# Neighbourhood attention: q and k split at their norm, loaded early, four pairs of heads in one sequence

## The chip, the core and the metric

The kernel runs on one core of a Trainium2 chip. The core has a matrix engine (TensorE, PE in the profile, with its weight loads as PEld), a vector engine (VectorE, DVE), a scalar engine (ScalarE, ACT), GpSimd (POOL) and a queue for transfers (SyncE, SP). Each engine works through its own instructions in order and waits for the others at semaphores. The metric is the device time of one execution in microseconds (us), the median of several runs.

## What is computed

Two layers of a hybrid block over 1024 latent tokens (a grid of 16 rows and 64 columns) and 256 context tokens, width 1024, float32. Each layer projects the normed tokens to three branches, runs them, and merges them with gates:

```
h = rms_norm(x, norm_w) * (1 + scale) + shift
(na_q, na_k, na_v, gla_q, gla_k, gla_v, gla_g, ret_q, ret_k, ret_v, z, g) = split_cols(h @ w_in)
na  = neighbourhood_attention(rms_norm(q), rms_norm(k), v, ...)     # 8 heads of 64
gla = bidir_scan(...)   # gated linear attention, 4 heads
ret = bidir_scan(...)   # retention, 4 heads
x = x + gate * merge_branches((na, gla, ret), z, g, w_branch, w_out)
```

In neighbourhood attention each latent token scores 8 rows by 16 columns of keys around it, with a bias from a table, and all 256 context keys, under one softmax:

```
s_win = einsum('bhwd,bhrwcd->bhwrc', q_r, k_win) * scale + bias
s_ctx = einsum('bhwd,bhnd->bhwn', q_r, kc) * scale
p = softmax(concat([s_win, s_ctx]))
o = einsum(p_win, v_win) + einsum(p_ctx, vc)
```

Context tokens attend to the context only; the last layer leaves their output out.

## The kernel before

**Slots.** A class `Drv` (L47) writes the program slot by slot. In each slot it moves the workers on by a step, emits a stretch of projection matmuls (the gemm stream), emits the stores deferred from the slot before and the evacuations of finished products, moves each lane on by a step, and the workers once more. A lane is one long generator, here the attention lane of a layer: retention, then GLA (`gla`, L627), then neighbourhood attention (`na`, L842). A worker is a short one, such as one unit of attention. A stretch has 6144 moving columns times `drv.mult` (L363, L374). So the order on each engine is fixed when the program is written, and a matmul that waits holds all matmuls behind it.

**Products in parts.** A product of float32 operands is made of three fast ones: hi by hi, hi by lo and lo by hi, where hi is the operand cast to the fast format and lo is the operand minus hi. `conv` (L330) splits weights: a cast on ACT (L337), two subtractions on POOL (L340).

**The q and k projections.** `fm` writes a product with 128 features on the partitions and up to 512 tokens in a row, in units of 24 matmuls (12,288 columns at 512 tokens). `qk_evac` (L1129) takes such a product of one pair of heads: copy and square on ACT (L1132, L1133), mean by a matmul (L1138), an inverse root on ACT (L1140 to L1142) with one Newton step on DVE (L1145 to L1160), where the tokens are also put into the order that attention reads. The result `raw` is stored to nq or nk in DRAM (m is 0 for q, 1 for k). There are 24 such evacuations in layer 0 and 20 in layer 1. They run while the lane is in GLA, whose decay differences dd are made on POOL (L775, L776), exponentiated on ACT (L789), multiplied on DVE (L798 to L800) and used by PE (L811). The tiles `nraw`, `nsq`, `nrs` come from `stg` (L144), a ring of eight buffers that the stores of the other stages share.

**Attention.** `na` takes the eight heads as four pairs. `load_v(p)` (L849) fetches the values of a pair into `vw` (four column windows, all row groups) and `vcx` (context). `heads(p)` (L860) first splits q and k of the pair at `drv.mult` 0.3 (`NA_M0`): for each head and each block of 512 or 256 tokens it loads 64 features of k and of q into a tile `nsp`, twice, to partitions 0 to 63 and 64 to 127 (a source with a leading broadcast of two), casts both to hi on ACT (L876) and subtracts on DVE (L879, L881), so that `ks` holds hi of k in both halves, `kl` lo of k, and `qs` hi of q in one half and lo of q in the other. One matmul over 128 partitions (L902) then gives hi by hi plus lo by hi, and one over 64 (L905) adds hi by lo. The lane waits until all of the pair is split (`lane_join(sp)`, L891). I call this the join. `qs`, `ks` and `kl` have one buffer each.

Then the units run at `drv.mult` 0.65, one spawned every second slot: eight windows of 128 latent tokens and, in layer 0, two blocks of context tokens. A unit (`pair`, L969) loads its bias `bt` (two buffers), makes the scores of its two heads (L902, L905), the softmax (DVE and ACT, L920 to L938), transposes the weights (L947, L950), copies them out (L961, L964), multiplies with the values (L999) and copies the result to `oN`, which is stored after four units.

While the lane runs attention, the gemm stream makes the gates g, whose results are stored by `gd<-st_g`.

Of the kernel before, what the change touches and what calls it, by code (L numbers as in the profile page):

```python
# [8 lines left out]
F32 = mybir.dt.float32  # L9
# [25 lines left out]
NA_M0, NA_M1 = 0.3, 0.65  # L35
# [11 lines left out]
class Drv:  # L47
    """Interleaves background work with the stream of projection matmuls, slot by slot."""
# [58 lines left out]
def hybrid_kernel(ctx: ExitStack, tc: tile.TileContext, A: dict, out: bass.AP):  # L107
# [39 lines left out]
    # ------------------------------------------------------------------ activations in hi/lo parts  # L147
# [29 lines left out]
    # ------------------------------------------------------------------ modulation  # L177
# [68 lines left out]
    # ------------------------------------------------------------------ norm of one token tile  # L246
# [47 lines left out]
    # ------------------------------------------------------------------ weights and projections  # L294
# [124 lines left out]
    # ================================================================== layers  # L419
    xcur = [A["x"][t * P:(t + 1) * P, :] for t in range(LT)] + [A["ctx"][t * P:(t + 1) * P, :] for t in range(2)]  # L420
    L = []
    for layer in range(DEPTH):
# [31 lines left out]
        d["nq"] = dt_("nq", [512, NTOK])  # L454
        d["nk"] = dt_("nk", [512, NTOK])
# [5 lines left out]
    # ------------------------------------------------------------------ retention / GLA output tail (one chunk)  # L461
# [43 lines left out]
    # ------------------------------------------------------------------ retention  # L505
# [120 lines left out]
    # ------------------------------------------------------------------ GLA  # L626
# [214 lines left out]
    # ------------------------------------------------------------------ neighbourhood attention  # L841
    def na(layer):  # L842
        d = L[layer]
        ntok, last = d["ntok"], d["last"]
        with tc.tile_pool(name=f"na{layer}", bufs=2) as pn:
            ws = []
            vts = {}

            def load_v(p):  # L849
                vw = pn.tile([P, 16, P], F32, tag="vw", name="vw", bufs=2)  # L850
                vcx = pn.tile([P, 2, P], F32, tag="vcx", name="vcx", bufs=2)
                vts[p] = vw, vcx
                nv = d["nv"][:, p * P:(p + 1) * P]
                for j in range(4):
                    dma(vw[0:4 * NCOL[j], j * 4:j * 4 + 4, :],
                        nv[0:NLAT, :].rearrange("(g c r) d -> (c r) g d", g=4, r=4)[4 * COL0[j]:4 * COL0[j] + 4 * NCOL[j], :, :])
                    yield
                dma(vcx, nv[NLAT:NTOK, :].rearrange("(c p) d -> p c d", p=P))

            def heads(p):  # L860
                drv.mult = NA_M0
                vw, vcx = vts[p]

                def split(hd, t0, nn):
                    hs = slice(64 * hd, 64 * hd + 64)
                    os = slice(64 - 64 * hd, 128 - 64 * hd)
                    pieces = []
                    for src, dst, on in ((d["nk"], ks[hd], True), (d["nq"], qs[hd], t0 < ntok)):
                        if on:
                            st = stg("nsp")  # L870
                            dma(st[:, :nn], src[p * P + 64 * hd:p * P + 64 * hd + 64, t0:t0 + nn].unsqueeze(0).to_broadcast([2, 64, nn]))
                            pieces.append((st, dst[:, t0:t0 + nn]))
                    yield
                    yield
                    for st, dst in pieces:
                        sc.copy(dst, st[:, :nn])  # L876
                    yield
                    yield
                    ve.tensor_tensor(kl[hs, t0:t0 + nn], pieces[0][0][hs, :nn], fv(pieces[0][1][hs]), op=ALU.subtract)  # L879
                    for st, dst in pieces[1:]:  # L880
                        ve.tensor_tensor(dst[os], st[os, :nn], fv(dst[os]), op=ALU.subtract)  # L881

                qs = [pn.tile([P, ntok], F32R, tag=f"q{x}", name=f"q{x}", bufs=1) for x in range(2)]
                ks = [pn.tile([P, NTOK], F32R, tag=f"k{x}", name=f"k{x}", bufs=1) for x in range(2)]
                kl = pn.tile([P, NTOK], F32R, tag="kl", name="kl", bufs=1)
                sp = []
                for t0, nn in blocks(NTOK):
                    for hd in range(2):
                        sp.append(drv.spawn(split(hd, t0, nn)))
                        yield  # L890
                yield from lane_join(sp)  # L891
                yield
                drv.mult = NA_M1
                nxt = load_v(p + 1) if p < 3 else iter(())

                def scores(qc, win):
# [3 lines left out]
                    def prod(outs, kof):  # L900
                        for hd in range(2):
                            pe.matmul(outs[hd], qs[hd][:, qc:qc + P], kof(ks[hd][:]), start=True, stop=False)  # L902
                        for hd in range(2):
                            hs = slice(hd * 64, hd * 64 + 64)
                            pe.matmul(outs[hd], qs[hd][hs, qc:qc + P], kof(kl[hs]), start=False, stop=True)  # L905
# [47 lines left out]
                def evac_t(hd, pts, win):  # L953
# [4 lines left out]
                    if win is not None:  # L958
                        half, j = win
                        cw = 4 * NCOL[j]  # L960
                        ve.tensor_copy(PT[0:cw, 0:384], ptw[0:cw, 0:384])  # L961
                        for i in range(3):
                            ch.append((vw[0:cw, j * 4 + half + i, hs], PT[0:cw, i * P:(i + 1) * P]))
# [5 lines left out]
                def pair(qc, win, dst, after):  # L969
                    bts = [None, None]  # L970
# [10 lines left out]
                    sc_ = scores(qc, win)  # L981
                    yield
                    ps_ = [soft1(sc_[hd], win, bts[hd]) for hd in range(2)]
                    yield
# [8 lines left out]
                    cA, cB = [evac_t(hd, ts[hd], win) for hd in range(2)]  # L993
# [12 lines left out]
                for half in range(2):  # L1006
                    oN = stg("oN")
                    for j in range(4):
# [5 lines left out]
                        ws.append(drv.spawn(pair((half * 4 + j) * P, (half, j), dst, after)))  # L1014
                        yield
                        if half or j > 1:
                            next(nxt, None)
                        yield
                if not last:
                    oN = stg("oNc")  # L1020
                    for cb in range(2):
# [4 lines left out]
                        ws.append(drv.spawn(pair(NLAT + cb * P, None, oN[:, cb * P:(cb + 1) * P], after)))  # L1026
                        yield
                        yield

            drv.mult = NA_M0  # L1030
            yield from load_v(0)
            for p in range(4):
                yield from heads(p)
# [3 lines left out]
    # ------------------------------------------------------------------ projections of one layer  # L1037
# [29 lines left out]
    def projections(layer):  # L1067
# [61 lines left out]
        def qk_evac(p):  # L1129
            def f(m, t0, nn, ps):  # L1130
# [4 lines left out]
                def w():  # L1135
# [25 lines left out]
                    dst = d["nq"] if m == 0 else d["nk"]  # L1161
                    drv.defer(lambda: dma(dst[p * P:(p + 1) * P, t0:t0 + nn], raw[:, :nn]))
# [53 lines left out]
    # ------------------------------------------------------------------ merge and output projection  # L1216
# [116 lines left out]
    # ------------------------------------------------------------------ background lane of one layer  # L1333
# [244 lines left out]
```

## Time and profile before

| | us |
|---|---|
| median of 3 runs | 3232.21 |
| lowest and highest run | 3231.21, 3236.86 |
| span of the profiled execution (first to last instruction) | 3228.6 |
| PE busy in it | 2914.7 |
| DVE, ACT, POOL busy in it | 1518.7, 1065.5, 1006.4 |
| attention stage, layer 0 | about 830 to 1322 |
| attention stage, layer 1 | about 2466 to 2900 |

The profile gives no time of the profiled execution besides its span, which is 3.6 us below the median of the runs. Its rows name an instruction by line, engine and operation, with output and inputs by the names above; `nsp<-nk` is a load of k into the split's tile. A timeline row begins with the start and the duration in us; "x16" is a run of 16 like instructions. SPq is SyncE's queue; a long SPq row is a transfer that could not be handed on at once. The granted clock is that of PE, as a share of full speed.

### The profile page before, as it was taken

To read this page: it belongs to the slowest core of one execution; us is meant where nothing else is said; L and a number is where in the kernel's file an instruction comes from. 1 tells how busy PE (TensorE), PEld (TensorE's weight loads), DVE (VectorE), ACT (ScalarE), POOL (GpSimd) and SP (SyncE) were. 2 spreads that over 40 slices of the span, in tenths; PEclk is the share of its full clock that TensorE was granted. 3 is DMA by queue.
4 is the path that set the end of the run, shared out by engine and by line. 5 is a ranking of instruction groups with operands and counts; after the bars stand their busy time and mean duration, and the time that the engine had idled before them with its cause. 6 is when DMAs were issued, how large, how long until landed. Compare 5 with 4: busy or idle time off the path is not lost.

```text
span 3228.6 us, 49602 instructions
## 1 busy us (share of the span) xinstructions
PE 2914.7 (90%) x18768; PEld 2481.6 (77%) x18768; DVE 1518.7 (47%) x3325; ACT 1065.5 (33%) x2459; POOL 1006.4 (31%) x962
## 2 busy tenths in 40 slices
PE   7999999899586787999999999999998677799999
PEld 5999977788475575777899999987776555577889
DVE  5046578666153354223434236477662444452331
ACT  4123565332143343221113222465332333332220
POOL 4122124455000011242655232124542010024474
PEclk9999999999898898999999999999999888899999
DMA  5244423323233233466435344432332333244633
GB/s 223 90 149 131 146 89 95 102 86 97 81 101 105 74 107 111 144 188 217 155 114 154 96 148 124 142 104 89 113 98 89 105 110 104 85 124 157 211 127 115
DMA packets 343887, 395.39 MB, mean 122 GB/s; under 512 B 28044, under 2 KB 259996, under 8 KB 343648
## 3 DMA queue, kind: packets, MB, share of 16 engines
q1 hardware_dynamic: 343648, 392.22, 38.4%
q8 instruction: 148, 2.42, 0.3%
q14 instruction: 91, 0.75, 0.1%
HBM read 289.54 MB, written 102.58 MB: 121 GB/s over the span
## 4 chain that ended last, share of the span: by engine, by line
PE 72%; DMA 10%; DVE 6%; issue 4%; SPq 4%; POOL 3%; ACT 1%; POOLq 0%; DVEq 0%; ACTq 0%
PE fm L371 30%; PE tm L371 17%; PE mg L371 9%; DMA nsp<-nk 5%; SPq L114 4%; PE gla_lv L811 3%; DMA nsp<-nq 3%; PE na_o L999 2%; PE na_ptw L947 1%; DVE ek L798 1%; DVE eq L799 1%; POOL wlo L340 1%; PE na_sc L902 1%; DVE eq L800 1%; PE na_ptc L950 1%
## 5 line engine op out<-in xcount | busy, mean ns | idle before, releaser
L371 PE MATMUL fm<-h,whi 128*128 128x512 f32 (+1 forms) x3936 | 942.6, 385 | 0.0
L340 POOL TENSOR_TENSOR wlo<-wraw,whi 128x512 fp32r<-128x512 f32 (+1 forms) x336 | 450.6, 1362 | 1415.2 <-ACT whi L337 1345.1
L371 PEld LDWEIGHTS fm<-h,whi 128*128 128x128 f32 x3936 | 685.5, 193 | 153.2 <-issue 29.4
L371 PE MATMUL fm<-h,wlo 128*128 128x512 f32 (+1 forms) x1968 | 472.6, 378 | 0.0
L371 PEld LDWEIGHTS fm<-h,wlo 128*128 128x128 f32 x1968 | 342.9, 191 | 69.1 <-issue 4.3
L371 PE MATMUL tm<-whi,h 128*128 128x256 f32 (+1 forms) x2528 | 346.6, 285 | 2.4 <-ACT h L290 1.7
L371 PEld LDWEIGHTS tm<-whi,h 128*128 128x128 f32 x2528 | 320.7, 189 | 4.0 <-ACT h L290 2.1
L337 ACT CAST whi<-wraw 128x1024 fp32r<-128x1024 f32 (+1 forms) x168 | 175.6, 1048 | 244.4 <-PE tm L371 121.1
L811 PE MATMUL gla_lv<-eq,ek 128*128 128x128 f32 x1008 | 138.3, 281 | 52.1 <-DVE eq L800 51.7
L811 PEld LDWEIGHTS gla_lv<-eq,ek 128*128 128x128 f32 x1008 | 128.2, 193 | 73.8 <-issue 45.7
L775 POOL TENSOR_TENSOR dd<-Ac,ash 128x256 f32<-128x256 f32 x126 | 106.6, 846 | 245.6 <-DVE eq L800 87.5
L371 PE MATMUL tm<-wlo,h 128*128 128x256 f32 (+1 forms) x1264 | 178.1, 283 | 0.0
L371 PEld LDWEIGHTS tm<-wlo,h 128*128 128x128 f32 x1264 | 163.0, 189 | 0.2 <-POOL wlo L340 0.2
L1175 ACT ACTIVATE st_g<-fm 128x512 f32<-128x512 f32 (+1 forms) x120 | 66.3, 553 | 277.1 <-PE fm L371 275.5
L371 PE MATMUL tm<-whi,yy 128*128 128x256 f32 x1152 | 148.1, 280 | 0.0
L371 PEld LDWEIGHTS tm<-whi,yy 128*128 128x128 f32 x1152 | 140.8, 188 | 0.1
L817 DVE COPY_PREDICATED att<-gmask,gla_lv 128x512 f32<-128x512 uint8 x108 | 80.0, 741 | 126.1 <-PE gla_lv L811 126.1
L1191 DVE SCALAR_TENSOR_TENSOR st_z<-st_z,fm 128x512 f32<-128x512 f32 (+1 forms) x60 | 38.0, 633 | 211.7 <-ACT st_z L1190 209.8
L902 PE MATMUL na_sw<-k,q 128*128 128x288 f32 (+1 forms) x128 | 39.7, 381 | 97.3 <-ACT k L876 97.3
L879 DVE TENSOR_TENSOR kl<-nsp,k 64x512 fp32r<-64x512 f32 (+1 forms) x48 | 29.5, 615 | 195.0 <-ACT k L876 195.0
L902 PE MATMUL na_sc<-k,q 128*128 128x256 f32 x144 | 41.6, 361 | 82.5 <-ACT k L876 82.4
L411 DVE COPY st_tm<-tm 128x256 f32<-128x256 f32 (+1 forms) x59 | 25.2, 428 | 171.9 <-PE tm L371 167.6
(1567 smaller groups left out, 4707.1 us busy)
## 6 DMA issues: line engine op xcount, KB each, us to landing
wraw<-in_w_in SPq DMA_DIRECT2D x104, 512.0 KB
wt<-in_w_mod SPq DMA_DIRECT2D x48, 512.0 KB
gd<-st_g SPq DMA_DIRECT2D x96, 256.0 KB
gt<-gd SPq DMA_DIRECT2D x96, 256.0 KB
bt<-in_na_bm SPq DMA_DIRECT2D x32, 384.0 KB
ot<-o SPq DMA_DIRECT2D x48, 256.0 KB
wraw<-in_w_branch SPq DMA_DIRECT2D x24, 512.0 KB
ret<-st_tm SPq DMA_DIRECT2D x78, 128.0 KB
```

Of the source, the lines that this page charges most:

```text
L114: nc.sync.dma_start(dst, src)
L337: sc.copy(hi[:, :, :w], raw[:, :, :w])
L340: gp.tensor_tensor(lo[:, ks, :w], raw[:, ks, :w], fv(hi[:, ks, :w]), op=ALU.subtract)
L371: pe.matmul(ps, a(k), b(k), start=i == 0, stop=i == tot - 1)
L775: gp.tensor_tensor(dv[:, :, Lh:], av[:, :, Lh:], rv, op=ALU.subtract)
L798: ve.tensor_tensor(ek_, E_, kd_, op=ALU.mult)
L811: pe.matmul(pl_[:, h, :], ek_[:, h, :], eq_[:, h, :], start=True, stop=True)
L817: ve.copy_predicated(att, gmask[:, lv, :].unsqueeze(1).to_broadcast([P, 4, P]), pl_)
L902: pe.matmul(outs[hd], qs[hd][:, qc:qc + P], kof(ks[hd][:]), start=True, stop=False)
L999: pe.matmul(po[64 * hd:64 * hd + 64, 0:P], ch[i][0], ch[i][1], start=i == 0, stop=i == n - 1)
L1175: sc.activation(st[:, :nn], ps, AF.Tanh, scale=0.5)
L1191: ve.scalar_tensor_tensor(st[:, :nn], st[:, :nn], 1.0, ps, op0=ALU.add, op1=ALU.mult)
```

## The change

The split moves from attention to `qk_evac`. After the Newton step the result is cast to hi on ACT into the tile of `rs`, POOL subtracts it to lo in place in `raw`, and the parts are stored: for q a tensor of [pair, head, 128, tokens] with hi in the head's own 64 rows and lo in the others (four stores), for k one tensor of hi and one of lo (two stores). Two steps lie between the Newton step and the stores that were not there.

`heads` no longer splits. k of a pair is loaded whole: `k0` and `k1`, each with the leading broadcast of two over 64 rows of 1280 tokens, and `kl` without one, two buffers each. q is loaded by each unit, 128 tokens of both heads, three buffers. The values of a window are loaded by each unit too, after its scores, in the three row groups that it uses, four buffers; before, 16 groups were loaded a pair and are shared by two units. `both(p)` loads k and vcx of a pair: the first pair's before any unit, seven slots at the multiplier that GLA leaves (1.0), those of pair p + 1 after units 3, 4 and 5 of pair p. There is no join; units of all four pairs follow each other, one every second slot, at 0.65.

```diff
-        d["nq"] = dt_("nq", [512, NTOK])
-        d["nk"] = dt_("nk", [512, NTOK])
+        d["nq"] = dt_("nq", [4, 2, P, NTOK])
+        d["nkh"] = dt_("nkh", [512, NTOK])
+        d["nkl"] = dt_("nkl", [512, NTOK])
...
+            def load_k(p):
+                ks = []
+                for hd in range(2):
+                    k = pn.tile([P, NTOK], F32R, tag=f"k{hd}", name=f"k{hd}", bufs=2)
+                    r = p * P + 64 * hd
+                    dma(fv(k[:]), d["nkh"][r:r + 64, :].unsqueeze(0).to_broadcast([2, 64, NTOK]))
+                    ks.append(k)
+                    yield
+                kl = pn.tile([P, NTOK], F32R, tag="kl", name="kl", bufs=2)
+                dma(fv(kl[:]), d["nkl"][p * P:(p + 1) * P, :])
+                tiles["k", p] = ks, kl
...
-                sp = []
-                for t0, nn in blocks(NTOK):
-                    for hd in range(2):
-                        sp.append(drv.spawn(split(hd, t0, nn)))
-                        yield
-                yield from lane_join(sp)
-                yield
-                drv.mult = NA_M1
-                nxt = load_v(p + 1) if p < 3 else iter(())
...
+                def load_vw(win):
+                    half, j = win
+                    cw = 4 * NCOL[j]
+                    vw = pn.tile([P, 3, P], F32, tag="vw", name="vw", bufs=4)
+                    dma(vw[0:cw], d["nv"][0:NLAT, p * P:(p + 1) * P].rearrange("(g c r) d -> (c r) g d", g=4, r=4)
+                        [4 * COL0[j]:4 * COL0[j] + cw, half:half + 3, :])
+                    return vw
...
                 def pair(qc, win, dst, after):
+                    q = pn.tile([P, 2, P], F32R, tag="q", name="q", bufs=3)
+                    dma(fv(q[:]), d["nq"][p, :, :, qc:qc + P].rearrange("h d t -> d h t"))
...
-            drv.mult = NA_M0
-            yield from load_v(0)
+            for _ in both(0):
+                yield
+            for _ in range(4):
+                yield
+            drv.mult = NA_M1
             for p in range(4):
-                yield from heads(p)
+                nxt = both(p + 1) if p < 3 else iter(())
+                for n, unit in enumerate(heads(p)):
+                    ws.append(drv.spawn(unit))
+                    yield
+                    if n > 2:
+                        next(nxt, None)
+                    yield
+                for _ in nxt:
+                    pass
...
-                    dst = d["nq"] if m == 0 else d["nk"]
-                    drv.defer(lambda: dma(dst[p * P:(p + 1) * P, t0:t0 + nn], raw[:, :nn]))
+                    hi, lo = rs.bitcast(F32R)[:, :nn], raw.bitcast(F32R)[:, :nn]
+                    yield
+                    sc.copy(hi, raw[:, :nn])
+                    yield
+                    gp.tensor_tensor(lo, raw[:, :nn], rs[:, :nn], op=ALU.subtract)
+
+                    def store():
+                        ts = slice(t0, t0 + nn)
+                        if m == 0:
+                            for hd in range(2):
+                                hs, os = slice(64 * hd, 64 * hd + 64), slice(64 - 64 * hd, 128 - 64 * hd)
+                                dma(d["nq"][p, hd, hs, ts], fv(hi[hs]))
+                                dma(d["nq"][p, hd, os, ts], fv(lo[hs]))
+                        else:
+                            dma(d["nkh"][p * P:(p + 1) * P, ts], fv(hi))
+                            dma(d["nkl"][p * P:(p + 1) * P, ts], fv(lo))
+                    drv.defer(store)
```

The transfers on SyncE, before, at the first join of layer 0 (wraw is a weight half, gd the store of a gate):

```order
L114 DMA nsp_8569<-nk_0_106 128x1x512
L114 DMA nsp_8571<-nq_0_105 128x1x512
L114 DMA nsp_8579<-nk_0_106 128x1x512
L114 DMA nsp_8581<-nq_0_105 128x1x512
L114 DMA wraw45_8583<-in_w_in 128x4x256
L114 DMA gd_0_99<-st_g_8561 128x256
L114 DMA nsp_8594<-nk_0_106 128x1x512
L114 DMA nsp_8596<-nq_0_105 128x1x512
L114 DMA nsp_8606<-nk_0_106 128x1x512
L114 DMA nsp_8608<-nq_0_105 128x1x512
```

Two more pairs of 256 tokens follow; the pair's first scores stand on PE after the first of these loads and need all of the tiles. After the change, on SyncE, from the bias of unit 3 to that of unit 5 of the first pair:

```order
L114 DMA bt<-in_na_be 128x2x288 [waits DMAHW2_49,DVE_49]
L114 DMA k_9007<-nkh_106 128x1x1280 [waits DMAHW3_49]
L114 DMA gd_99<-st_g 128x512 [waits DMAHW4_49,Activation_49]
L114 DMA vw<-nv_104 96x3x128 [waits DMAHW5_49]
L114 DMA q<-nq_105 128x2x128 [waits DMAHW6_49,PE_49]
L114 DMA bt<-in_na_be 128x2x288 [waits DMAHW7_49,DVE_49]
L114 DMA wraw_9075<-in_w_in 128x4x256 [waits DMAHW0_49,Pool_49]
L114 DMA gd_99<-st_g 128x256 [waits DMAHW1_49,Activation_49]
L114 DMA k_9100<-nkh_106 128x1x1280 [waits DMAHW2_49]
L114 DMA vw<-nv_104 96x3x128 [waits DMAHW3_49,PE_49]
L114 DMA q<-nq_105 128x2x128 [waits DMAHW4_49,PE_49]
L114 DMA bt<-in_na_bm 128x2x384 [waits DMAHW5_49,DVE_49]
```

The loads of the next pair's k now stand among the loads of the running units, and a transfer waits for the one eight issues earlier (the counters DMAHW0 to DMAHW7 are used in turn): the second vw here waits for the first k.

PE at the change of pairs in layer 1, before, from the last scores of the first pair (fm is the gemm stream, na_ptw and na_ptc the transposes, na_o the values' product):

```order
L371 MATMUL fm<-h_4_16236,wlo_23913 128x512 x4
L371 MATMUL fm<-h_0_16239,whi_23778 128x512 x4
L902 MATMUL na_sw<-k_24389,q_24387 128x288
L902 MATMUL na_sw<-k_24390,q_24388 128x288
L905 MATMUL na_sw<-kl,q_24387 128x288
```

After it:

```order
L371 MATMUL fm<-h_4_16285,wlo_23930 128x512 x4
L985 MATMUL na_o<-PT,vw 64x128 x6
L985 MATMUL na_o<-PT,vcx 64x128 x4
L877 MATMUL na_sw<-k_24106,q 128x288
L877 MATMUL na_sw<-k_24199,q 128x288
```

Before, 26,624 columns of gemm stand between the last scores of one pair and the first of the next, and the last units have run out; now 8,192 stand there, as between any two units, and the unit before last of the old pair is still on its way.

POOL in the q and k stage of layer 0, before:

```order
L775 TENSOR_TENSOR dd<-Ac_5549,ash 128x64x4
L776 TENSOR_TENSOR dd<-ash,Ac_5549 128x64x4
L340 TENSOR_TENSOR wlo_5809<-wraw_5602,whi_5808 128x2x256 x2
L775 TENSOR_TENSOR dd<-Ac_5549,ash 128x128x2
L776 TENSOR_TENSOR dd<-ash,Ac_5549 128x128x2
```

After it:

```order
L1160 TENSOR_TENSOR nraw<-nraw,nrs 128x512
L776 TENSOR_TENSOR dd<-Ac_5595,ash 128x64x4
L777 TENSOR_TENSOR dd<-ash,Ac_5595 128x64x4
L1160 TENSOR_TENSOR nraw<-nraw,nrs 128x256
L340 TENSOR_TENSOR wlo_5867<-wraw_5649,whi_5866 128x2x256 x2
L776 TENSOR_TENSOR dd<-Ac_5595,ash 128x128x2
L777 TENSOR_TENSOR dd<-ash,Ac_5595 128x128x2
L1160 TENSOR_TENSOR nraw<-nraw,nrs 128x512 x2
```

The new subtractions (L1160 in the changed file, whose lines from there on are numbered differently) stand between GLA's.

More of the change, by code (lines that the diff above doesn't have):

```diff
@@ L34 @@
 GL_M = (1.1, 1.2, 1.0)
-NA_M0, NA_M1 = 0.3, 0.65
+NA_M1 = 0.65
 BR_ORDER = (2, 1, 0)
@@ L846, in na @@
             ws = []
-            vts = {}
+            tiles = {}
+            def load_k(p):
[9 more added lines that the diff above has]
+                tiles["k", p] = ks, kl
@@ L849, in load_v @@
             def load_v(p):
-                vw = pn.tile([P, 16, P], F32, tag="vw", name="vw", bufs=2)
                 vcx = pn.tile([P, 2, P], F32, tag="vcx", name="vcx", bufs=2)
[L852 to L856, printed above, removed]
-                    yield
@@ L858, in load_v @@
-                dma(vcx, nv[NLAT:NTOK, :].rearrange("(c p) d -> p c d", p=P))
-            def heads(p):
-                drv.mult = NA_M0
[L862 to L872, printed above, removed]
-                    yield
[L874 to L885, printed above, removed]
-                sp = []
-                for t0, nn in blocks(NTOK):
-                    for hd in range(2):
-                        sp.append(drv.spawn(split(hd, t0, nn)))
-                        yield
-                yield from lane_join(sp)
-                yield
-                drv.mult = NA_M1
-                nxt = load_v(p + 1) if p < 3 else iter(())
-                def scores(qc, win):
@@ L897, in scores @@
+                tiles["v", p] = vcx
+                dma(vcx, d["nv"][NLAT:NTOK, p * P:(p + 1) * P].rearrange("(c p) d -> p c d", p=P))
+                yield
+            def heads(p):
+                (ks, kl), vcx = tiles["k", p], tiles["v", p]
+                def scores(q, win):
                     psc = [psa("na_sc") for _ in range(2)]
@@ L980, in pair @@
                     yield
-                    sc_ = scores(qc, win)
+                    sc_ = scores(q, win)
                     yield
                     ps_ = [soft1(sc_[hd], win, bts[hd]) for hd in range(2)]
+                    vw = load_vw(win) if win is not None else None
                     yield
@@ L992, in pair @@
                     yield
-                    cA, cB = [evac_t(hd, ts[hd], win) for hd in range(2)]
+                    cA, cB = [evac_t(hd, ts[hd], win, vw) for hd in range(2)]
                     yield
@@ L1013, in after @@
                                 dma(d["o"][0][p * P:(p + 1) * P, 512 * half:512 * half + 512], oN)
[L1014 to L1018, printed above, removed]
+                        yield pair((half * 4 + j) * P, (half, j), dst, after)
                 if not last:
@@ L1025, in after, with both @@
                                 dma(d["o"][0][p * P:(p + 1) * P, NLAT:NTOK], oN[:, 0:256])
[L1026 to L1030, printed above, removed]
-            yield from load_v(0)
-            for p in range(4):
-                yield from heads(p)
+                        yield pair(NLAT + cb * P, None, oN[:, cb * P:(cb + 1) * P], after)
+            def both(p):
+                yield from load_k(p)
+                yield from load_v(p)
+            for _ in both(0):
[3 more added lines that the diff above has]
+            drv.mult = NA_M1
+            for p in range(4):
+                nxt = both(p + 1) if p < 3 else iter(())
[7 more added lines that the diff above has]
+                    pass
             yield from lane_join(ws)
```

9 lines of the change are left out of this document (5 added, 4 removed).

## The prediction

> **What bounds the kernel now.** I read the page first: the engines' shares and the chain that ended last.
>
> ```profile
> span 3228.6 us, 49602 instructions
> PE 2914.7 (90%) x18768; PEld 2481.6 (77%) x18768; DVE 1518.7 (47%) x3325; ACT 1065.5 (33%) x2459; POOL 1006.4 (31%) x962
> PE 72%; DMA 10%; DVE 6%; issue 4%; SPq 4%; POOL 3%; ACT 1%; POOLq 0%; DVEq 0%; ACTq 0%
> ```
>
> TensorE (PE) is busy for 2914.7 of 3228.6 us, so 314 us of idleness is all that any reordering can win, besides matmuls that run on a low clock. The second share in the chain is DMA with its queue, 14%, and the chain's lines name the loads of nk and nq into nsp. The table of waits says who sits idle for them (columns: us in total, times, longest).
>
> ```profile
> PE na_sw L902 <- ACT k L876: 97.3, 10, 20.2
> PE na_sc L902 <- ACT k L876: 82.4, 16, 7.0
> ACT k L876 <- DMA nsp<-nk: 162.9, 42, 8.6
> ```
>
> The scores wait on the hi copies, and the hi copies on the loads. Then I cut the attention stages into windows: the eight stretches in which a pair of heads is split, and one stretch of units between two of them (us, PE busy, PEld, DVE, ACT, POOL, granted clock, DMA share, GB/s).
>
> ```profile
> 840.00:900.00 60.00, 18.89 (x85) 14.85 (x84) 6.77 (x12) 8.57 (x17) 2.55 (x2) 0.65 0.24 80
> 900.00:967.00 67.00, 67.00 (x478) 53.46 (x478) 41.54 (x138) 31.35 (x103) 7.73 (x6) 0.98 0.31 99
> 967.00:1018.00 51.00, 23.98 (x105) 18.20 (x104) 9.02 (x20) 11.17 (x26) 2.50 (x2) 0.70 0.26 87
> 1087.00:1132.00 45.00, 21.06 (x86) 16.40 (x87) 6.62 (x12) 7.95 (x17) 2.29 (x2) 0.70 0.22 79
> 1188.00:1248.00 60.00, 32.41 (x178) 25.07 (x175) 14.60 (x37) 13.88 (x35) 2.60 (x2) 0.74 0.23 80
> 2475.00:2536.00 61.00, 22.64 (x85) 17.06 (x84) 10.46 (x24) 10.33 (x22) 2.52 (x2) 0.66 0.25 84
> 2587.00:2632.00 45.00, 25.46 (x124) 19.24 (x123) 13.25 (x31) 11.59 (x30) 2.99 (x2) 0.75 0.31 102
> 2673.00:2730.00 57.00, 37.90 (x197) 28.31 (x196) 21.82 (x53) 17.04 (x46) 5.22 (x4) 0.79 0.26 91
> 2771.00:2830.00 59.00, 36.92 (x200) 27.97 (x198) 18.74 (x53) 14.94 (x41) 2.52 (x2) 0.80 0.24 79
> ```
>
> Length minus PE busy gives 41.1, 27.0, 23.9 and 27.6 us in layer 0 and 38.4, 19.5, 19.1 and 22.1 us in layer 1: 218.7 us. Between the joins PE is full (67.00 of 67.00). So two thirds of all idleness of PE lies in the eight joins.
>
> **The joins go.** The gemm columns are the same before and after, 4,783,104 of them counted on PE, so work that no longer runs inside a join runs elsewhere on a full PE, and what is saved is the idleness: 218.7 us. With it goes the restart on a low clock. PE's rows right before and right after the first join, same tiles:
>
> ```profile
> 839.30 2.04 PE L371 MATMUL fm<-h,whi 128*128 128x256 f32 x16
> 841.18 1.10 PE L371 MATMUL fm<-h,wlo 128*128 128x256 f32 x8
> 898.01 3.78 PE L371 MATMUL fm<-h,whi 128*128 128x256 f32 x16
> 901.59 1.53 PE L371 MATMUL fm<-h,wlo 128*128 128x256 f32 x8
> ```
>
> 1.74 and 0.43 us more, 2.2 us a join, 17 us for eight. Gross gain 236 us. The Trainium skill (TensorE: Matmul & The Clock Gate, "Part 1: The HAM clock gate") says that the first 3.4 us or so after idleness run at half clock, which by itself would make it 1.7 us a restart and the gross gain 4 us smaller; the trace's 2.2 us is used.
>
> The casts (L876) and halved subtractions (L879, L881) that leave the attention stage leave engines that are not its bound: nothing.
>
> **The new k loads.** Their form is that of the nsp loads: a leading broadcast of two. SyncE's rows (SPq, issue time) and the window give its price.
>
> ```profile
> 869.78 4.98 SPq L114 DMA_DIRECT2D nsp<-nq  x1
> 874.86 4.98 SPq L114 DMA_DIRECT2D nsp<-nk  x1
> 879.93 4.99 SPq L114 DMA_DIRECT2D nsp<-nq  x1
> ...
> 862.00:873.00 11.00, 0.00 (x0) 0.00 (x0) 0.86 (x2) 0.70 (x2) 0.00 (x0) 0.50 0.13 50
> ```
>
> One load of 256 KB every 5.1 us, 50 GB/s, and a DMA share of 0.13 of 16 engines: two engines work, fourteen are idle. A k load moves 640 KB, so 2.5 times 5.1 us, 12.8 us on two engines, 25.6 us a pair of heads, and each later transfer has a share on those two and ends behind it. The Trainium skill has the rule (DMA: Bandwidth & Descriptors, "Rules for kernel authors"): a leading zero-stride broadcast of c copies confines the DMA to c engines. It speaks against this form, and the trace agrees, 0.13 being 2 of 16. By the same page's fit for an unconfined load ("Anatomy of one DMA", 2.0 us plus bytes at 436 GB/s) a k load would take an estimated 3.5 us and the stalls below would vanish.
>
> How much of it PE sees depends on the lead. Three units of the first pair:
>
> ```profile
> 911.70 0.63 PE L902 MATMUL na_sw<-k,q 128*128 128x384 f32 x2
> 914.66 0.37 SPq L114 DMA_DIRECT2D bt<-in_na_be  x1
> 919.64 0.54 PE L902 MATMUL na_sw<-k,q 128*128 128x288 f32 x2
> 927.43 0.54 PE L902 MATMUL na_sw<-k,q 128*128 128x288 f32 x2
> ```
>
> A unit every 7.9 us; the bias load of a unit goes out when the softmax two units earlier lets its buffer go, 3.0 us after those scores. In the new order the first k load stands right behind the bias load of unit 3. Let that be t = 0: scores of unit 1 were at -3.0, those of unit 5 come at 28.6. The first k is through at 12.8. The loads issued between (vw, q, bt, a weight half, gd stores) put 3 to 5 us on the same two engines, at 25 GB/s and a sixteenth of 0.1 to 0.5 MB each. The second k ends at about 30. The q of unit 5 stands behind it and takes some 3 us more (one small load took 4.2 us in the row below). It lands at 33, 4.4 us late. Where fewer loads lie between (layer 1) it is some 3 us. I take 4 us for each of six prefetches, 24 us; the ends are 0 and 13 us (all of one k load seen). kl and vcx follow at about 35, and the next pair's first scores are not before 52: no join is left there.
>
> ```profile
> 397.01 4.19 DMA qkw<-in_na_qkw
> ...
> 446.93 5.56 PE fm L371 x24
> ...
> 827.73 0.60 PE L480 MATMUL post_t<-ident,pon 128*128 128x128 f32 x4
> 829.08 0.37 SPq L114 DMA_DIRECT2D o<-pof  x1
> ```
>
> The first pair of each layer: between the last post_t and the first scores stand 71,680 gemm columns, 5.83 units of 12,288, at 5.56 us each 32.4 us: scores due at 860. k goes out after that store of pof, at 829.5; two k (25.6), about 5 us of other loads and 3 for q make 863. Some 4 us late in each layer, 8 us; ends 0 and 12 each. PE restarts cold after some of these eight stalls: 10 us. New waits: 24 + 8 + 10 = 42 us.
>
> **The split at the norm.** Each of 44 evacuations gets an ACT cast (L876 takes 0.55 us for a tile), a POOL subtraction, and two or four stores where there was one. The price of the subtraction and what it does to VectorE (DVE) beside it:
>
> ```profile
> L340 POOL TENSOR_TENSOR wlo<-wraw,whi 128x512 fp32r<-128x512 f32 (+1 forms) x336 | 450.6, 1362 | 1415.2 <-ACT whi L337 1345.1 <-DMA bt<-in_na_be 45.6 <-DMA A<-Ac 24.5
> L876 ACT CAST k<-nsp 128x512 fp32r<-128x512 f32 (+1 forms) x48 | 26.3, 549 | 162.9 <-DMA nsp<-nk 162.9
> 439.87 1.09 DVE L1156 SCALAR_TENSOR_TENSOR nraw<-nsq,nrs 128x256 f32<-128x256 f32 x2
> 446.32 2.80 POOL L340 TENSOR_TENSOR wlo<-wraw,whi 128x512 fp32r<-128x512 f32 x2 [20.45 <-ACT whi L337]
> 446.87 2.74 DVE L1156 SCALAR_TENSOR_TENSOR nraw<-nsq,nrs 128x256 f32<-128x256 f32 x2
> ...
> 440.00:460.00 20.00, 20.00 (x105) 16.27 (x104) 19.33 (x49) 12.29 (x21) 4.83 (x4) 1.00 0.32 98
> 560.00:580.00 20.00, 13.67 (x75) 11.24 (x76) 17.38 (x32) 11.79 (x20) 6.73 (x6) 0.91 0.42 122
> ```
>
> On POOL it stands ahead of GLA's dd in the queue and waits for the cast. While POOL subtracted two tiles, the same two DVE operations took 2.74 us and not 1.09: 0.8 us a tile. So 44 x 0.8 = 35 us on DVE and 44 x 0.55 = 24 us on ACT; nothing of it reaches PE if all is hidden, 59 us if nothing is. DVE at 19.33 of 20 us left PE full in one slice, and at 17.38 PE lost 6 us in another. I take a quarter, 15 us. The stores are 84 more issues on SyncE at 0.37 us (the store of pof above), 31 us on a queue that is no bound; behind them stand GLA's loads of kd, qd and vt, which are fetched a chunk ahead, so I cost them at nothing; without that cover it is within the 59 us. The q and vw loads of each unit are two more issues, with the lead shown above.
>
> **The sum.** 3228.6 - 236 + 42 + 15 = 3049.6 us of span. The median of the runs, 3232.2, is 3.6 us above this span; so 3053 us.
>
> **Rivals.** *The two engines bind* (0.19): every prefetch shows one whole k load, 6 x 13, the first pairs 2 x 12, 20 us of cold restarts and 15 for the split: 137 us, 3133 us. For it: 25.6 us of each pair's 63 us (eight units) are taken on two engines that also carry their share of the rest, 0.31. Against it: the lead of two units above.
> *All is hidden* (0.10): no new wait, split free: 3232 - 236 = 2996 us.
> *The staging ring* (0.04, the slower side): raw and rs now both stay taken until stores have landed that go out one slot later, and an evacuation takes three of the ring's eight buffers; ACT, waiting to write a buffer, holds the queue in which PE's banks are emptied. If each of the 44 waits one slot of gemm, 5.56 us, that is 245 us: 3232 - 236 + 42 + 245 = 3283. It decides from 194 / 44 = 4.4 us each. Against it: now ACT hardly waits for such stores, 0.7 us in all.
>
> ```profile
> L1132 ACT COPY nraw<-fm 128x512 f32<-128x512 f32 (+1 forms) x44 | 23.0, 523 | 27.8 <-PE fm L371 27.0 <-DMA nk<-nraw 0.7
> ```
>
> *The join stays*, because the next pair's k is not there in time: it would need another 17 us of delay, from 35 to 52; it counts with the first rival.
>
> **Numbers.** The forecast has 0.65, with 3005 to 3110 from its bounds; the first rival (0.19) spreads from there to 3180 and is taken in up to 3130; of the second (0.10) the upper half is taken in, down to 3000; the ring has 0.04, and 0.02 is left for a time within 0.2%, where gains and new waits cancel. The range 3000 to 3130 leaves out about 2 in 10. A measurement tells 0.2%, 6.5 us, from no change. Faster 0.94, same 0.02, slower 0.04.
>
> **What would show it.** Right: no nsp rows; PE's idleness in both attention stages under 60 us instead of 219, and what is left waits on q or k loads, about unit 5 of a pair; DMA share near 0.13 plus the rest while k loads run; PE's idleness in the stage of the q and k projections up by 10 to 20 us. Wrong: waits of ACT nraw or nsq on DMA of tens of us (the ring), or scores that wait 10 us and more at each prefetch (the two engines).

## The result, and the profile after

The changed kernel takes 3090.6 us (median of 4 runs, 3089.2 to 3092.5) against 3231.9 us before (median of 4): a ratio of 0.956, interval 0.9546 to 0.9573. The forecast was 3053 us, from 3000 to 3130. The gain is 141 us and not 179.

The page of the changed kernel, its span and its engines:

```profile
span 3089.2 us, 49961 instructions
PE 2904.9 (94%) x18768; PEld 2476.7 (80%) x18768; DVE 1488.8 (48%) x3237; ACT 1044.3 (34%) x2415; POOL 1061.4 (34%) x1006
```

PE's idleness, span less busy time, fell from 314 to 184 us. The table of waits names what is left (us in total, times, longest):

```profile
PE gla_lv L812 <- DVE eq L801: 75.0, 49, 5.5
PE na_sw L877 <- DMA q<-nq: 57.6, 8, 10.4
```

The second row is new: the scores wait for the q load in eight places, the two first pairs and the six prefetches. The first row, GLA's matmuls waiting for VectorE's product `eq`, was shorter before:

```profile
PE gla_lv L811 <- DVE eq L800: 51.7, 39, 4.3
```

To see where the time came from, both traces are cut at the same work: at the first mean of squares of the q and k norms (na_ms) and at GLA's last transpose (post_t) of each layer. The order of matmuls up to these marks is the same, so the pieces compare. First before, then after (us, PE busy, PEld, DVE, ACT, POOL, granted clock, DMA share, GB/s). Rows 2 and 4 are the stage of norms and GLA, rows 3 and 5 everything from the end of GLA to the next such mark, the attention stage in front.

```profile
0.00:414.90 414.90, 392.98 (x3107) 360.38 (x3108) 191.86 (x465) 147.73 (x333) 109.70 (x110) 1.00 0.45 146
414.90:828.10 413.20, 386.78 (x2264) 330.04 (x2262) 283.31 (x478) 175.24 (x368) 176.88 (x198) 0.99 0.30 92
828.10:2118.60 1290.50, 1158.60 (x7910) 999.60 (x7908) 516.27 (x1281) 384.38 (x939) 351.54 (x314) 0.95 0.41 130
2118.60:2464.00 345.40, 319.51 (x1714) 263.78 (x1713) 236.81 (x402) 149.75 (x300) 152.08 (x167) 1.00 0.31 96
2464.00:3228.60 764.60, 656.81 (x3783) 527.76 (x3781) 290.45 (x701) 208.38 (x522) 216.22 (x174) 0.92 0.39 126
```

```profile
0.00:415.30 415.30, 390.50 (x3107) 360.02 (x3108) 191.88 (x465) 147.72 (x333) 109.70 (x110) 0.97 0.46 146
415.30:852.30 437.00, 394.30 (x2264) 333.27 (x2262) 291.76 (x478) 186.11 (x392) 204.91 (x222) 0.98 0.33 99
852.30:2051.00 1198.70, 1151.89 (x7909) 996.48 (x7907) 500.98 (x1233) 361.88 (x891) 352.60 (x314) 0.98 0.47 144
2051.00:2415.80 364.80, 324.76 (x1715) 266.26 (x1714) 247.31 (x402) 159.46 (x320) 177.81 (x187) 0.99 0.35 103
2415.80:3089.20 673.40, 643.45 (x3783) 520.66 (x3781) 256.89 (x661) 189.16 (x482) 216.37 (x174) 0.97 0.48 149
```

The attention pieces became 91.8 and 91.2 us shorter, 183 us. The norm and GLA stages became 23.8 and 19.4 us longer, 43 us. The difference, with 0.4 us at the start, is the gain of 139.4 us of span.

The waits in PE's own rows, three of the eight (start, us, and in brackets the idle time and what ended it):

```profile
891.79 0.82 PE L877 MATMUL na_sw<-k,q 128*128 128x288 f32 x2 [6.74 <-DMA q<-nq]
939.28 0.98 PE L877 MATMUL na_sw<-k,q 128*128 128x384 f32 x2 [7.64 <-DMA q<-nq]
...
1112.23 0.98 PE L877 MATMUL na_sw<-k,q 128*128 128x384 f32 x2 [10.42 <-DMA q<-nq]
```

The first is the first pair of layer 0; the others stand at about the sixth unit of a pair ("unit 5" of the prediction, which counts from 0). The matmuls behind them are slow: two scores of 384 columns take 0.98 us here and took 0.63 us on the full clock before. Two windows behind the first stall show how long that lasts:

```profile
891.79:898.60 6.81, 6.81 (x18) 4.96 (x19) 3.68 (x14) 2.53 (x9) 0.00 (x0) 0.50 0.62 198
898.70:902.00 3.30, 3.30 (x16) 2.29 (x15) 0.74 (x3) 0.00 (x0) 0.00 (x0) 0.99 0.79 268
```

So by an estimate from these windows (half of 6.81 us) a stall of 6.74 us costs some 3.4 us more in slow matmuls.

### The profile page after: what moved, and what is told of

Its sections match the earlier page's. It is cut to its first block, busy times and chain, and to the rows that moved or that the text cites. A ratio compares the mean times of both kernels' runs of the same rounds, so it can differ in the third digit from the quotient of the medians.

```text
span 3089.2 us, 49961 instructions
## 1 busy us (share of the span) xinstructions
PE 2904.9 (94%) x18768; PEld 2476.7 (80%) x18768; DVE 1488.8 (48%) x3237; ACT 1044.3 (34%) x2415; POOL 1061.4 (34%) x1006
## 5 line engine op out<-in xcount | busy, mean ns | idle before, releaser
L371 PE MATMUL fm<-h,whi 128*128 128x512 f32 (+1 forms) x3936 | 926.8, 381 | 0.0
L799 DVE TENSOR_TENSOR ek<-dd,kd 128x512 f32<-128x512 f32 x108 | 98.7, 914 | 29.9 <-ACT dd L790 26.8
L1322 DVE TENSOR_TENSOR st_o<-tm,gb 128x256 f32<-128x256 f32 x72 | 30.5, 424 | 155.8 <-PE tm L371 135.0
L1268 DVE SCALAR_TENSOR_TENSOR gt<-gt,mg 128x512 f32<-128x512 f32 (+1 forms) x80 | 50.7, 634 | 110.9 <-PE mg L371 93.2
```

Of the source, the lines that this page charges most:

```text
L371: pe.matmul(ps, a(k), b(k), start=i == 0, stop=i == tot - 1)
L799: ve.tensor_tensor(ek_, E_, kd_, op=ALU.mult)
L1268: ve.scalar_tensor_tensor(gt[:, :nn], gt[:, :nn], 1.0, ps[:, :nn], op0=ALU.add, op1=ALU.mult)
```

## The experiments

Two questions: what makes the scores wait (k loads on two DMA engines, or loads that go out too late), and what makes the norm stage longer (the cast and the subtraction, or the stores and the ring of staging buffers). A third came out of the first answers: how much of the old joins was their order at all. Ratios are against the kernel before, run beside each batch.

**Plain k loads.** The changed kernel with

```
-  dma(fv(k[:]), d["nkh"][r:r + 64, :].unsqueeze(0).to_broadcast([2, 64, NTOK]))
+  for x in range(2):
+      dma(fv(k[64 * x:64 * x + 64]), d["nkh"][r:r + 64, :])
```

> Only the k loads differ from the changed kernel: each head's 64 rows are loaded twice by two plain loads, one for each half of the tile, instead of once with a leading broadcast of two. Theory (two engines): the waits of the scores on q and k, 57.6 us in eight places in the changed kernel, come from k loads confined to two DMA engines, and fall under 15 us; 3091 - 45 = about 3046 us, and the DMA share while a k load runs is no longer near 0.13. Rival (the lead or SyncE's order): the loads go out too late or queue behind others whatever engines they use; the waits stay over 35 us and the time stays at 3080 or more.

Measured: 3012.1 us, ratio 0.9311 (0.9297 to 0.9325). Its windows, cut as above, and the stretch from the first scores to the last output of layer 0's attention:

```profile
415.30:854.70 439.40, 395.23 (x2264) 334.28 (x2262) 291.78 (x478) 186.43 (x392) 205.19 (x222) 0.98 0.33 98
854.70:2010.50 1155.80, 1141.82 (x7910) 990.09 (x7907) 499.40 (x1233) 361.33 (x891) 353.32 (x314) 1.00 0.49 149
2010.50:2377.30 366.80, 329.47 (x1716) 270.31 (x1714) 246.72 (x402) 159.54 (x320) 177.52 (x187) 0.97 0.35 103
2377.30:3012.30 635.00, 630.83 (x3783) 512.17 (x3781) 255.98 (x661) 188.89 (x482) 216.58 (x174) 1.00 0.52 158
```

```profile
887.30:1188.00 300.70, 300.70 (x2131) 236.85 (x2131) 183.96 (x579) 137.31 (x451) 32.91 (x25) 1.00 0.50 148
```

PE is busy for 300.70 of 300.70 us. In layer 1 it is 255.20 of 255.20. Of the waits for q 0.2 us is left, in one place. The attention pieces are 42.9 and 38.4 us shorter than in the changed kernel, 81 us, where its waits were 57.6: the other 24 us go with the slow matmuls behind them (PE busy in the two pieces falls from 1795.3 to 1772.7 us, for the same matmuls). The expectation of 3046 counted the waits alone. The confined loads show in the changed kernel's trace too, SyncE's rows and a window at layer 1's first pair:

```profile
2418.09 1.15 SPq L114 DMA_DIRECT2D k<-nkh  x2
2419.33 10.74 SPq L114 DMA_DIRECT2D wraw<-in_w_in  x1
```

```profile
2420.00:2430.00 10.00, 10.00 (x45) 8.11 (x44) 0.00 (x0) 2.13 (x3) 2.54 (x2) 1.00 0.12 50
```

Two engines at work (0.12 of 16), 50 GB/s, and a weight load that SyncE needs 10.74 us to issue behind them. With plain loads SyncE issues two of them in 1.1 us, and a window with the second k of a prefetch in layer 1 stands at a DMA share of 0.84:

```profile
2424.00:2430.00 6.00, 6.00 (x38) 4.69 (x39) 4.84 (x16) 2.82 (x10) 0.00 (x0) 1.00 0.84 237
```

The two-engine cause is shown; the rival, lead alone, is out: the loads go out in the same places of the order, and the waits are gone.

**No split at the norm.** The changed kernel without the lines `sc.copy(hi, ...)` and `gp.tensor_tensor(lo, ...)`; the unsplit value `raw` is stored in both places. The stores are the same; `rs` is no longer held until they land.

> Leaves out the cast to hi and the subtraction of lo at the norm: the unsplit value is stored in both places, by the same stores one slot later, out of the same ring of buffers. Theory (hand-offs): the 43 us by which the norm and GLA stages grew (413.2 to 437.0 us and 345.4 to 364.8 us) come from ACT's cast and POOL's subtraction, which wait in the queues ahead of GLA's operations; both stages return to within 5 us of the kernel before, and the time is about 3091 - 38 = 3053 us. Rival (stores and ring): the longer hold of the ring's buffers or the 84 more stores cost it; then the stages stay over 430 and 359 us and the time at 3080 or more.

Measured: 3047.7 us, ratio 0.942 (0.9405 to 0.9436). The two stages:

```profile
414.90:828.60 413.70, 386.78 (x2264) 330.10 (x2262) 282.88 (x478) 175.19 (x368) 176.49 (x198) 0.99 0.35 105
2025.50:2371.10 345.60, 319.55 (x1714) 263.58 (x1713) 237.08 (x402) 149.77 (x300) 151.83 (x167) 1.00 0.36 109
```

Both stages are back where the kernel before had them (413.2 and 345.4 us), and so is PE's wait for `eq`, 51.7 us before and 75.0 in the changed kernel:

```profile
PE gla_lv L812 <- DVE eq L801: 52.4, 40, 4.4
```

The 84 more stores and the steps ahead of them cost nothing here. The 43 us go with the cast and the subtraction. That `rs` is freed earlier in this run leaves the ring as a rival; the changed kernel's own waits answer it (below, under the rivals).

**Without the subtraction.** Only the `gp.tensor_tensor` line left out.

> Leaves out only POOL's subtraction (the unsplit value is stored as the lo part); ACT's cast stays. If it is POOL's place in GLA's path (its subtractions wait 86.9 us for casts, ahead of GLA's differences): 25 to 30 us come back, about 3063 us. If it is ACT's place (the casts wait 80 us for VectorE, ahead of GLA's exponentials): under 12 us come back, 3080 or more.

Measured: 3072.1 us, ratio 0.9496 (0.9481 to 0.951).

```profile
415.20:839.80 424.60, 391.51 (x2262) 332.80 (x2261) 283.73 (x478) 186.22 (x392) 176.37 (x198) 0.98 0.35 102
2039.80:2397.30 357.50, 323.90 (x1714) 265.54 (x1713) 237.97 (x402) 159.30 (x320) 153.63 (x167) 0.99 0.35 106
```

Of the 43 us, 23.5 stay with the cast alone and 19.7 go with POOL's subtraction: neither of the two answers, ACT or POOL, but both, about half and half when the subtraction is the one left out. VectorE's busy time in the two stages, 291.76 and 247.31 us in the changed kernel, is back at 283.73 and 237.97 without POOL's subtractions.

**The split on VectorE.** The same values, made on another engine:

```
-  sc.copy(hi, raw[:, :nn])
-  yield
-  gp.tensor_tensor(lo, raw[:, :nn], rs[:, :nn], op=ALU.subtract)
+  ve.tensor_copy(hi, raw[:, :nn])
+  ve.tensor_tensor(lo, raw[:, :nn], rs[:, :nn], op=ALU.subtract)
```

> The same result as the changed kernel: hi and lo are both made on VectorE, in one slot, right behind the multiplication that makes the value; no hand-off to ACT and POOL. VectorE gets 44 casts and 44 subtractions more, about 2 x 44 x 0.55 = 48 us. Theory (hand-offs): the waits in ACT's and POOL's queues go, 20 to 30 us come back, about 3066 us. Rival (VectorE's load): GLA's operations on VectorE are late by the added work, no gain, 3085 us or more.

Measured: 3077.4 us, ratio 0.9517 (0.9501 to 0.9532).

```profile
415.20:845.20 430.00, 392.97 (x2263) 333.42 (x2262) 309.30 (x526) 175.06 (x368) 179.14 (x198) 0.98 0.34 101
2051.00:2409.20 358.20, 325.42 (x1716) 267.44 (x1714) 260.49 (x442) 149.76 (x300) 156.27 (x167) 0.98 0.36 105
```

13.6 of the 43 us come back, fewer than the 20 to 30 expected: without any hand-off 29.6 us remain, with 26.0 and 23.7 us more work on VectorE than in the two stages of the kernel before (283.31 and 236.81 us). So the work costs without a hand-off too. (The profiled execution is 6.8 us above the median of this run; the gain by the medians, 13.2 us, agrees with that of the stages.)

**The kernel before with plain loads.** In its join:

```
-  dma(st[:, :nn], src[p * P + 64 * hd:p * P + 64 * hd + 64, t0:t0 + nn].unsqueeze(0).to_broadcast([2, 64, nn]))
+  for x in range(2):
+      dma(st[64 * x:64 * x + 64, :nn], src[p * P + 64 * hd:p * P + 64 * hd + 64, t0:t0 + nn])
```

> The kernel before, with one edit: in the join each 64-row piece of q and k is loaded twice by plain loads, one for each half of the staging tile, and not once with a leading broadcast. It asks how much of the eight joins (218.7 us idle, and what a low clock adds) was the two engines. Theory (the joins were made of loads on two engines): the idleness before the scores falls to under 100 us and the time to about 3235 - 150 = 3085 us. Rival (the joins are bound by their order: staging buffers, casts and halved subtractions one after another): less than 60 us come back, over 3175 us.

Measured: 2982.4 us, ratio 0.9223 (0.9209 to 0.9237): these two lines alone do better than the whole change. Its windows, cut as above:

```profile
415.30:828.70 413.40, 386.83 (x2264) 329.92 (x2262) 282.62 (x478) 175.28 (x368) 177.04 (x198) 0.99 0.30 92
828.70:1988.80 1160.10, 1142.34 (x7910) 988.49 (x7909) 516.52 (x1281) 383.50 (x939) 351.83 (x314) 1.00 0.47 145
1988.80:2334.30 345.50, 321.01 (x1714) 264.87 (x1713) 237.28 (x402) 149.73 (x300) 152.06 (x167) 0.99 0.32 96
2334.30:2978.60 644.30, 635.38 (x3783) 514.31 (x3781) 288.89 (x701) 207.57 (x522) 216.37 (x174) 1.00 0.48 149
```

The attention pieces are 1804.4 us, against 2055.1 before and 1790.8 in the changed kernel with plain k loads. Of the 264 us between the first and the last of these, 251 go with the form of the loads alone, and 13.6 are left for the order without a join. The join's loads now go out at 1.2 us a pair, at a DMA share of 0.82 and not 0.13:

```profile
842.22 1.12 SPq L114 DMA_DIRECT2D nsp<-nk  x2
843.38 1.38 SPq L114 DMA_DIRECT2D nsp<-nq  x2
```

```profile
840.00:853.90 13.90, 13.90 (x73) 11.58 (x71) 2.76 (x5) 5.02 (x8) 2.54 (x2) 1.00 0.82 235
```

**The cast a slot later**, on top of plain k loads: one more `yield` ahead of `sc.copy(hi, ...)`.

> The kernel with plain k loads (3012 us), and ACT's cast one slot later, so that VectorE has had a slot more to finish the value. Theory (waiting in queues): the cost of the split is ACT's queue waiting for VectorE (50, 31 and 31 us of waits before the cast) and POOL's for ACT; most of it goes and 15 to 25 us come back, about 2992 us. Rival (the work itself stands in GLA's chain, wherever in the slot it is): within 5 us of 3012.

Measured: 3018.2 us, ratio 0.9333 (0.9316 to 0.935), so no gain beside 0.9311. The waits of the cast for VectorE did go down, first with plain k loads alone and then here:

```profile
ACT nrs L1159 <- DVE nraw L1152: 50.4, 15, 6.9
ACT nrs L1159 <- DVE nraw L1146: 30.9, 14, 6.0
ACT nrs L1159 <- DVE nraw L1156: 30.6, 11, 3.6
```

```profile
ACT nrs L1160 <- DVE nraw L1156: 23.2, 10, 4.2
ACT nrs L1160 <- DVE nraw L1152: 22.5, 9, 5.6
ACT nrs L1160 <- DVE nraw L1146: 9.9, 5, 4.1
```

From 112 us to 56, and the time did not fall. But the run moved waits more than it removed them: all waits of ACT at the norm's tiles (the rows of nraw, nsq and nrs in the two stages) went from 136 to 147 us, those for the evacuations' own stores among them from 7 to 24. So it doesn't decide between the two. That the work costs something without any wait for another engine rests on the run with the split on VectorE, with its 29.6 us; how the 43 us divide between work and waits stays open.

**The split on POOL**, on top of plain k loads: `gp.tensor_copy(hi, raw[:, :nn])` for the cast and the subtraction right behind it.

> The kernel with plain k loads (3012 us), and both the cast and the subtraction on POOL. ACT is free of the split; POOL gets 44 casts more, ahead of GLA's differences. If ACT's place is the dearer one (with POOL's subtraction left out 23.6 of 43 us stayed, on ACT alone): about 10 us come back, 3002. If what counts is the work ahead of GLA's differences on POOL: 10 to 25 us slower, 3022 to 3037.

Measured: 3004.7 us, ratio 0.929 (0.9275 to 0.9305). The interval meets that of plain k loads on ACT and POOL, 0.9311; 7 us better at the most likely, not told apart. It is not slower, as POOL's place in GLA's chain would have had it.

**Longer slots with the split on VectorE**, on top of plain k loads: `GL_M = (1.1, 1.4, 1.0)` for `(1.1, 1.2, 1.0)`, the factor by which a slot of matmuls between two steps of GLA is made longer.

> The kernel with plain k loads (3012 us), the split on VectorE in one slot (13 us less by the run before), and GLA's slots made longer while the q and k projections run, 1.4 for 1.2, so that more matmuls stand between two steps of GLA. If the stage loses time because GLA's chain through POOL, ACT and VectorE is longer than a slot, PE's idleness in it (30 us with the split on VectorE) falls by half and the time is about 2985 us. If the chain is not what PE waits for, GLA only ends later and the time is 2999 or more.

Measured: 2975.6 us, ratio 0.92 (0.9187 to 0.9214), 36 us less than with plain k loads alone. PE's wait for GLA's operands went from 73.2 us (plain k loads) to 46.0:

```profile
PE gla_lv L812 <- DVE eq L801: 46.0, 34, 4.0
```

That is below the 51.7 us of the kernel before, and this version does as well as the kernel before with plain loads. It fits the theory that a slot longer than GLA's chain takes up the work of the split. But the run changes two things at once, the engine of the split and the slots, and no run has the longer slots with the split on ACT and POOL; how much each gives is not shown.

**The prefetch two units earlier**, the broadcast left in: `if n > 0` for `if n > 2`.

> The changed kernel (3091 us), k loads with their broadcast as they are, but the prefetch of the next pair begins two units (16 us) earlier: after units 1, 2 and 3 instead of 3, 4 and 5. Theory (a backlog on two engines): two k loads issued 7.9 us apart put 25.6 us of work on the two engines within 16 us; the q of the unit behind them waits about as long wherever in the pair this happens; waits on q over 40 us, 3075 to 3095 us. Rival (the lead): the k loads go out too late, and 16 us more hide them: waits on q under 20 us, about 3030 us.

Measured: 3102.8 us, ratio 0.9601 (0.9585 to 0.9617), slower than the change, with its row of the waits for q:

```profile
PE na_sw L877 <- DMA q<-nq: 62.4, 11, 9.0
```

**The prefetch spread**, the broadcast left in: `if n in (1, 4, 6, 7)` for `if n > 2`.

> The changed kernel (3091 us), k loads with their broadcast, but spread over the pair: the first head's k after unit 1, the second's after unit 4, kl after unit 6. The second k and kl go out no earlier than in the changed kernel. Theory (a backlog on two engines): 24 us lie between two k loads of 12.8 us, so the two engines are free again before the second, and no q waits; only the two first pairs still wait (12.7 us of 57.6); waits under 25 us, about 3091 - 50 = 3041 us. Rival (the lead): no gain, or a new wait on kl; 3085 us or more.

Measured: 3041.8 us, ratio 0.9417 (0.9401 to 0.9433).

```profile
PE na_sw L877 <- DMA q<-nq: 22.5, 6, 6.9
```

An earlier prefetch doesn't help and a spread one does, with the second k no earlier than it was: what the q loads wait for is two k loads close behind each other on two engines.

**The kernel before with plain loads and longer slots**: `GL_M = (1.1, 1.4, 1.1)`, and then `(1.1, 1.5, 1.2)`.

> The kernel before with plain loads in its joins (2982 us), and GLA's slots longer: 1.4 for 1.2 while the q and k projections run, 1.1 for 1.0 after them. PE's idleness in the norm and GLA stages is 26.6 and 24.5 us there. If PE waits because GLA's chain is longer than a slot, half of it goes: about 2960 us. If not, 2980 or more.

> As the run with 1.4 and 1.1, with 1.5 and 1.2: about 2955 us if the idleness goes on falling with the length of a slot; back over 2965 if GLA then ends so late that attention has too few matmuls left beside it.

Measured: 2973.1 us, ratio 0.9203 (0.9189 to 0.9217), and 2995.3 us, 0.9268 (0.9251 to 0.9286). The first's interval meets that of plain loads alone (0.9223), so its 9 us are not told apart; GLA's wait on VectorE went from 50.7 to 34.6 us. The second is too far. The best versions, 2973 and 2976 us, are equal by their intervals and 8% under the kernel before.

## Why the prediction was right, and where it was off

The mechanism was right: the joins' idleness went, new waits on q came where they were placed, and the norm stage grew. The total came out 38 us short of the forecast gain: the gross gain was put 28 us too small, and the two costs 39 and 28 us too small. That 28 of the 67 us of cost were made up by an error of the other sign is luck. The bounds 3005 to 3110 are also narrower than the ends of the prediction's own terms, which add up to 2996 and 3167.

*The joins go, 236 us.* Measured 264 us, by the attention pieces with plain k loads (2055.1 less 1790.8). The idleness in it is as forecast: length less PE busy in the two attention pieces falls from 239.7 to 18.2 us, 221 for 218.7. The term that was too small is the restart: 17 us were put down, 43 measured (264 less 221, and PE busy in the two pieces is 1815.4 us before and 1772.7 with plain k loads). Windows of 1 us over the joins agree: PE's busy time, times what the clock lacks of 1.00, adds up to 21.3 us in layer 0 (828.1 to 1322) and 23.0 in layer 1 (2464 to 2900), and to 0.0 in both with plain k loads. The step counted one restart for each join, by the 24 matmuls behind it. One restart is somewhat longer, since the scores ahead of those run on the low clock as well. The kernel before, right after its first join:

```profile
897.00:902.50 5.50, 5.50 (x24) 5.05 (x25) 2.24 (x9) 1.29 (x4) 0.00 (x0) 0.50 0.49 175
```

That is 2.75 us lost and not 2.2. Above all, six of the eight joins, all but the first of each layer, hold a second restart: PE stops for the last softmax weights of the old pair (`PT`, which ACT copies out), and starts again on the low clock before the join is over. First the row of the waits, then the second join of layer 0, where eight matmuls take 3.78 us (four took 1.17 us right before the stop):

```profile
PE na_o L999 <- ACT PT L964: 38.6, 6, 9.3
```

```profile
982.59 1.39 PE L999 MATMUL na_o<-PT,vcx 128*64 128x128 f32 x8 [9.33 <-ACT PT L964]
983.91 3.78 PE L371 MATMUL fm<-h,whi 128*128 128x512 f32 x8
```

The few matmuls that run singly inside a join add the rest. The Trainium skill (TensorE: Matmul & The Clock Gate, "Part 1: The HAM clock gate") was drawn on for half clock during the first 3.4 us; 5.5 us here and 6.8 us in the changed kernel are longer, and the measurement decides.

*The new k loads, 42 us.* Measured 81 us: 44.9 us of waits at the six prefetches for 24, 12.7 at the two first pairs for 8, and 24 us of slow matmuls behind them for 10. The places were right, and so was the lead. In the first pair of layer 0 k goes out here:

```profile
903.43 0.52 SPq L114 DMA_DIRECT2D k<-nkh  x1
```

PE was done with what stands ahead of the scores of unit 5 at 931.64, 28.2 us later (28.6 in the prediction), and the scores ran at 939.28, 35.9 us later, where q was forecast for 33. So, as far as this place shows, the term that was too small is what the two engines had to do before that q, by some 3 us; no run took apart which transfers these were. The Trainium skill (DMA: Bandwidth & Descriptors, "Rules for kernel authors") says that a leading broadcast of two confines a transfer to at most two engines; the share of 0.12 agrees. The prediction's own estimate, by that page's fit ("Anatomy of one DMA"), was that unconfined loads make the stalls vanish. The page gives the fit for transfers issued by GpSimd, and these are issued by SyncE; the stalls did vanish, to 0.2 us.

*The split at the norm, 15 us.* Measured 43 us (43.2 in the two stages, and 0.7 without the split). The step that failed is "I take a quarter" of 59 us of added work. Nearly three quarters of that sum showed. In these stages PE waits for the end of GLA's chain from POOL over ACT to VectorE: by the windows PE's idleness there rose by 30.4 us, 23.3 of them in its wait for `eq` (51.7 to 75.0), and its busy time, the same matmuls on a lower clock, by 12.8. The sum itself was made up otherwise than forecast: by the windows VectorE's busy time rose by 19 us and not 35, ACT's by 21 for 24, and POOL's own 54 us of subtractions (28.0 and 25.7) were named as being in the queue, but not in the sum. Of these 93 us of work, a little under half reached PE.

*The rivals.* "Two engines bind" was the right mechanism for the excess: 7.2 us a place (57.6 by 8), between the 4 taken and its 12 to 13. "All is hidden" is out. "The staging ring" is out: it needed 194 us of ACT's waits for the evacuations' own stores, and the changed kernel has 7.1:

```profile
ACT nraw L1127 <- DMA nq<-nrs: 4.2, 1, 4.2
ACT nsq L1128 <- DMA nq<-nrs: 2.9, 1, 2.9
```

"The join stays" didn't come.

*What nobody priced.* The gross gain was put down to the end of the join. The prediction saw that the join's loads used two of 16 engines, cited the rule against the new loads, and did not turn it on the old ones: spread over all engines, the same loads in the same order leave 13.6 us of the 264. So nearly all that the change won by a new order, the form of the loads had cost. With plain loads on both sides the change is 30 us slower (3012.1 against 2982.4), since it pays 47.6 us at the norm (806.2 less 758.6) for those 13.6.

## What to carry to other kernels

Before work is moved so as to hide a transfer, look at the DMA share while it runs: 0.13 with a queue that issues nothing else means two engines, and the form of the load is the thing to mend. Work moved out of a stage where its engines wait has a price in the stage where it goes; ask there which chain PE waits for, and count a good part of the added work if it stands in that chain: here 43 of 93 us with the split on ACT and POOL, and 30 of 50 with it on VectorE. A stall of several us costs its length and, here, four tenths as much again on the low clock (24 us for 57.6); count the restarts inside a wait as well as the one behind it.

## What the hardware showed

Two broadcast loads held up more than themselves: PE waited 5.8 to 10.4 us for a q of 128 KB behind them on the same queue, and SyncE needed 10.74 us to issue the next load. Loading the same 64 rows twice, by two plain transfers, took 1.2 us of issue time for what had taken 5 in the middle of a join. After a stall of 6.74 us PE's clock was at 0.50 for 6.8 us more. POOL's 44 subtractions made VectorE's own work longer: the same 478 and 402 operations took 8.0 and 9.3 us more beside them than in the run without them.
